# Turning the result tiles of the last output projection on VectorE instead of TensorE

## The chip, the core and the metric

The kernel runs on one core of one Trainium2 chip. The metric is the device time of one execution in microseconds (us), as the median of several executions. The engines named below are TensorE (PE, with its weight loads shown apart as PEld), VectorE (DVE), ScalarE (ACT), GpSimd (POOL) and SyncE (SP). SP computes nothing here: it issues transfers (DMAs). ACT issues some as well.

## The reference, cut to what matters

One step of a two-layer decoder trunk on 1024 new prompt tokens and on 8 sample tokens. Layer 0 is a retention layer, layer 1 a sliding-window attention layer. Each layer ends with an output projection and a residual; the change concerns that of layer 1, which gives the outputs y_prompt and y_sample.

```python
def swa_layer(x, g_norm, w_in, q_gain, k_gain, sinks, w_out, k_buf=None, v_buf=None):
    B, L, _ = x.shape
    h = rmsnorm(x, g_norm)
    proj = h @ w_in
    q, k, v, gate = jnp.split(proj, [SWA_Q, SWA_Q + SWA_KV, SWA_Q + 2 * SWA_KV], axis=-1)
...
    o = o * jax.nn.silu(gate)
    return x + o @ w_out, new_k, new_v
```

Here x is 1024 x 1024 for the prompt and 8 x 1024 for the sample, and w_out is 1024 x 1024, all in fp32.

## The kernel before

**Tiles.** The gated branch output of the attention layer lies in the on-chip tensor `SA`, with features on the partitions and 1032 tokens (1024 of the prompt, 8 of the sample) along the free axis. Its product with w_out is made in 24 result tiles (ft, ti). ft counts eight groups of 128 output features, ti three groups of tokens, `TG` = 0 to 384, 384 to 768 and 768 to 1032; the last has 256 prompt and 8 sample tokens. `so_all` (L2173) takes the tiles in the order (0,0) to (5,0), (0,1) to (5,1), (0,2) to (5,2), then (6,0), (6,1), (6,2), (7,0), (7,1), (7,2).

**One tile.** `start` (L2177) asks for weights and for the residual, takes a PSUM buffer (`ms`, `pj` or `sc`) and issues the products of the first seven of eight k steps through `proj` (L1654); `finish` (L2209) issues those of the eighth. To keep fp32 precision every operand is split into a high and a low part, and each k step is three matmuls (L1661 high by high, L1662 high by low, L1663 low by high), so 24 matmuls a tile, with 128 features as outputs and the tile's 384 or 264 tokens as columns. Then `finish` adds the residual on DVE (L2217: `yt`, in a buffer named `sq` with two copies), lets `x_ahead` (L2195) issue the next load of a residual tile, and calls `so_y` for the tile before this one (`pend_y`).

**Turning and storing.** A result tile has features on the partitions, the output has tokens as rows. `so_y` (L2156) turns each 128 tokens by a matmul with the identity (`tr`, L105, into the PSUM buffer `tr`), three of them a tile of 384 tokens; a tile with ti = 2 has two of 128 and one for the 8 sample columns. ACT copies the result to SBUF (`yo`, L2166, and L2170 for the sample) and issues the store on its own queue (L2167 and L2171). Each row of that store is one run of 128 features, 512 bytes.

**Residuals.** `x_ahead` loads residual tile `xr2` on SP (L2205); where ti = 2 a second, small load brings the 8 sample columns (L2207, from `xdec`). Two buffers exist. The load for a tile can be issued when the add of the tile two before it has read its buffer.

**Weights.** `wslot` (L1638) loads 256 columns of w_out, that is the weights of two groups ft, in two halves of 512 KB on SP (L1647, into `wr`), and splits them: ACT writes the high part (`wh`, L1650), DVE at this place subtracts for the low part (`wl`, L1651). There are three buffers of `wh` and `wl` for four pairs of groups. The last pair (ft 6 and 7) therefore goes into the buffer of the first (ft 0 and 1), whose last reader is tile (1,2), six tiles and a part before its first use in (6,0).

**What sets the order.** PE's instructions stand in the order in which the program issues them. In this part of the kernel the order on DVE, ACT and SP is decided by a scheduler, which places instructions by its own estimates of when they can run; so an edit can move instructions that it doesn't name. On each engine, instructions and transfers are issued strictly in order: one that waits holds up all behind it. The hardware transfers raise eight semaphores in turn, and each transfer waits for the one that used its semaphore before, eight transfers earlier.

Of the kernel before, what the change touches and what calls it, by code (L numbers as in the profile page):

```python
# [7 lines left out]
F32 = mybir.dt.float32  # L8
F32R = mybir.dt.float32r
AF = mybir.ActivationFunctionType  # L10
# [60 lines left out]
def _trunk(ctx, tc, nc, a):  # L71
# [6 lines left out]
    y_p, y_s, nrp, nrs = a["y_p"], a["y_s"], a["nrp"], a["nrs"]  # L78
# [25 lines left out]
    def tr(out, in_, ident, start=True, stop=True):  # L104
        nc.tensor.matmul(out, in_, ident, is_transpose=True, start=start, stop=stop)  # L105


    ident = cp.tile([128, 128], F32, name="ident")
# [601 lines left out]
    t0 = 0.0  # L710
    for h in range(H):
        t0 = max(t0 + GAP, sets[3 * h + 2].end + 10.0)
# [209 lines left out]
    trp = ctx.enter_context(tc.tile_pool(name="trp", bufs=2, space=PSUM))  # L922
# [797 lines left out]
    atp = ctx.enter_context(tc.tile_pool(name="atp", bufs=1))  # L1720
# [115 lines left out]
    def dec_cache(hf):  # L1836

        pt = trp.tile([128, 512], F32, name="tr")
        for i in range(4):
            tr(pt[:, i * 128:i * 128 + 128], kcT["c"][:, 4 * hf + i, :], ident)  # L1840
        return pt
# [314 lines left out]
    def so_y(ft, ti, yt):  # L2156
        t0, t1 = TG[ti]
        npr = min(t1, NP) - t0
        nch = npr // 128
        pt = trp.tile([128, 512], F32, name="tr")  # L2160
        for i in range(nch):
            tr(pt[:, i * 128:i * 128 + 128], yt[:, i * 128:i * 128 + 128], ident)
        if ti == 2:
            tr(pt[:8, 256:384], yt[:, 256:264], ident)
        yo = atq[0].tile([128, 384], F32, tag="ot", name="yo", bufs=2)
        nc.scalar.activation(yo[:, :npr], pt[:, :npr], AF.Copy)  # L2166
        nc.scalar.dma_start(out=y_p[0, t0:t0 + npr, ft * 128:ft * 128 + 128].rearrange("(c p) f -> p c f", p=128),  # L2167
                            in_=yo[:, :npr].rearrange("p (c f) -> p c f", f=128))
        if ti == 2:
            nc.scalar.activation(yo[:8, 256:384], pt[:8, 256:384], AF.Copy)  # L2170
            nc.scalar.dma_start(out=y_s[:, 0, ft * 128:ft * 128 + 128], in_=yo[:8, 256:384])  # L2171

    def so_all():  # L2173
# [35 lines left out]
        def finish():  # L2209
            ft, ti, ps = early.pop(0)  # L2210
            held.discard(min(held))
            t0, t1 = TG[ti]
            n = t1 - t0
            proj(ps[:, :n], so_slots[ft // 2], ft % 2, t0, t1, first=False, last=True, ks=[7])
            yield 3 * n / 2400.0
            yt = io("sq", 2)
            nc.vector.tensor_tensor(yt[:, :n], ps[:, :n], xrs.pop(0)[:, :n], ALU.add)  # L2217
            x_ahead()
            if pend_y:
                so_y(*pend_y.pop(0))  # L2220
            pend_y.append((ft, ti, yt))
# [11 lines left out]
        while pend_y:  # L2233
            so_y(*pend_y.pop(0))
# [13 lines left out]
    out = so_all()  # L2248
# [53 lines left out]
    pt = dec_cache(0)  # L2302
# [4 lines left out]
    pt = dec_cache(1)  # L2307
# [100 lines left out]
```

## Time and profile before

| quantity | value |
| --- | --- |
| time, median of 3 runs | 1294.03 us (1293.03 to 1294.62) |
| the profiled execution's own time | 1293.47 us |
| its span in the profile | 1291.7 us |
| mean granted TensorE clock over the span | 0.996 of full speed |
| DVE, ACT, POOL busy over the span | 766.3, 668.2, 741.4 us |
| first and last add of the output projection (L2217) | 1182.4 and 1287.2 us |
| loads of residual tiles, 16 and 8 | 192 KB and 128 KB each, by SP |
| stores of result tiles, 16 and 8 | 192 KB and 128 KB each, by ACT |

Times in the trace are in us from the start of the span, and 1.8 us of the execution's own time lie outside it. A row of a timeline gives start, duration, engine, line, operation and output<-inputs; a bracket behind it is the idle time of that engine just before, and what ended it. PE's matmuls are pipelined: the distance from one start to the next says what one costs, not its duration.

### The profile page before, as it was taken

The page shows a single profiled execution, that of the slowest core. Times are in us where ns is not written, and L with a number is a line of the kernel's source. Part 1 is how long each engine was busy: PE and PEld are TensorE (multiplying, and loading weights), DVE is VectorE, ACT ScalarE, POOL GpSimd, SP SyncE. Part 2 cuts the span into 40 slices and gives each one's busy share as a digit, 9 for nine tenths or more (in the row PEclk, how much of TensorE's full clock was granted, in tenths as well). Part 3 has the DMA queues.
Part 4 walks back from the last instruction along what each step waited for, and adds up shares of the span by engine and source line. Part 5 has one row for each costly group of instructions (what it writes and reads, how often), then busy time and mean ns, then how long its engine had stood idle before and what let it go on. Part 6 is the DMA issues. An engine that isn't in the chain of part 4 may idle for free.

```text
span 1291.7 us, 26846 instructions
## 1 busy us (share of the span) xinstructions
PE 1268.1 (98%) x9839; PEld 1216.2 (94%) x9839; DVE 766.3 (59%) x1474; ACT 668.2 (52%) x1656; POOL 741.4 (57%) x886
## 2 busy tenths in 40 slices
PE   6999999999999999999999999999999999999998
PEld 5999999999999999988889999999999999998998
DVE  5954646665576764476763656855566666765321
ACT  5533445454555554588761234545575766765121
POOL 5654444535359899798771458636585767544000
PEclk9999999999999999999999999999998999999999
DMA  6313857677667673556879855833031221137232
GB/s 227 108 54 121 253 183 237 179 253 218 186 210 226 192 239 107 180 173 218 255 211 261 229 195 153 272 113 103 15 118 50 66 66 58 54 119 249 78 92 79
DMA packets 221967, 206.69 MB, mean 160 GB/s; under 512 B 32728, under 2 KB 196820, under 8 KB 221820
## 3 DMA queue, kind: packets, MB, share of 16 engines
q1 hardware_dynamic: 189840, 170.61, 43.8%
q10 hardware_dynamic: 31996, 34.36, 8.2%
q8 instruction: 78, 1.28, 0.4%
q14 instruction: 53, 0.43, 0.1%
HBM read 135.41 MB, written 70.55 MB: 159 GB/s over the span
## 4 chain that ended last, share of the span: by engine, by line
PE 90%; DVE 3%; DMA 2%; POOL 1%; ACT 1%; issue 1%; SPq 0%; ACTq 0%; DVEq 0%; POOLq 0%
PE b L335 8%; PE b L336 8%; PE b L337 8%; PE S L1302 7%; PE pj L1661 6%; PE pj L1662 6%; PE pj L1663 6%; PE b L328 4%; PE tr L105 4%; PE b L329 4%; PE b L330 4%; PE o L2023 2%; PE b L544 1%; PE sc L1986 1%; PE S L335 1%; PE S L336 1%
## 5 line engine op out<-in xcount | busy, mean ns | idle before, releaser
L335 PE MATMUL b<-xh,woh 128*128 128x258 f32 x784 | 223.2, 285 | 0.0
L337 PE MATMUL b<-xh,wol 128*128 128x258 f32 x784 | 221.7, 283 | 0.0
L336 PE MATMUL b<-xl,woh 128*128 128x258 f32 x784 | 221.6, 283 | 0.0
L1661 PE MATMUL pj<-SA,wh 128*128 128x384 f32 (+1 forms) x496 | 169.3, 341 | 1.5 <-ACT SA L2043 1.3
L1662 PE MATMUL pj<-SA,wh 128*128 128x384 f32 (+1 forms) x496 | 159.4, 321 | 0.2 <-DVE SA L2044 0.2
L1663 PE MATMUL pj<-SA,wl 128*128 128x384 f32 (+1 forms) x496 | 159.4, 321 | 0.0
L335 PEld LDWEIGHTS b<-xh,woh 128*128 128x128 f32 x784 | 148.0, 189 | 4.1 <-issue 3.7
L336 PEld LDWEIGHTS b<-xl,woh 128*128 128x128 f32 x784 | 148.7, 190 | 0.0
L337 PEld LDWEIGHTS b<-xh,wol 128*128 128x128 f32 x784 | 148.0, 189 | 0.0
L226 POOL TENSOR_TENSOR wol<-raw,woh 128x512 fp32r<-128x512 f32 x51 | 66.2, 1306 | 120.3 <-ACT woh L221 109.2
L328 PE MATMUL b<-woh,xh 128*128 128x256 f32 x448 | 126.6, 283 | 0.0
L329 PE MATMUL b<-wol,xh 128*128 128x256 f32 x448 | 126.0, 281 | 0.0
L330 PE MATMUL b<-woh,xl 128*128 128x256 f32 x448 | 125.6, 280 | 0.0
L1661 PEld LDWEIGHTS pj<-SA,wh 128*128 128x128 f32 x496 | 94.1, 190 | 5.1 <-issue 2.4
L1662 PEld LDWEIGHTS pj<-SA,wh 128*128 128x128 f32 x496 | 94.3, 190 | 0.4 <-DVE SA L2044 0.4
L2001 POOL TENSOR_TENSOR s<-s,sm 128x512 f32<-128x512 f32 x64 | 66.6, 1041 | 48.2 <-DVE sm L2000 43.2
L1663 PEld LDWEIGHTS pj<-SA,wl 128*128 128x128 f32 x496 | 93.9, 189 | 0.0
L328 PEld LDWEIGHTS b<-woh,xh 128*128 128x128 f32 x448 | 84.3, 188 | 5.0 <-issue 2.9
L330 PEld LDWEIGHTS b<-woh,xl 128*128 128x128 f32 x448 | 84.3, 188 | 0.0
L329 PEld LDWEIGHTS b<-wol,xh 128*128 128x128 f32 x448 | 84.3, 188 | 0.0
L1993 ACT ACTIVATE s<-s,mx 128x257 f32<-128x257 f32 x128 | 64.2, 505 | 34.9 <-DVE mx L1991 34.2
L221 ACT ACTIVATE woh<-s 128x512 fp32r<-128x512 f32 x88 | 54.1, 624 | 54.4 <-POOL s L211 20.7
(530 smaller groups left out, 3622.6 us busy)
## 6 DMA issues: line engine op xcount, KB each, us to landing
raw<-in_w_in_ret_dram ACTq DMA_DIRECT2D x44, 512.0 KB
st<-in_state_ret_dram SPq DMA_DIRECT2D x64, 256.0 KB
out_dram<-st SPq DMA_DIRECT2D x64, 256.0 KB
vb<-vscr SPq DMA_DIRECT2D x64, 128.0 KB
evp<-qks SPq DMA_DIRECT2D x32, 256.0 KB
evx<-vsc SPq DMA_DIRECT2D x32, 256.0 KB
wr<-in_w_in_swa_dram SPq DMA_DIRECT2D x32, 256.0 KB
evc<-gsc SPq DMA_DIRECT2D x16, 256.0 KB
```

The source lines that it names most:

```text
L226: eng.tensor_tensor(lo, src_of(s, name, sub), hi.bitcast(F32), SUB)
L328: mm(dst, xh, wh, start=a and i == 0, stop=False, skip_group_check=True)
L329: mm(dst, xh, wl, start=False, stop=False, skip_group_check=True)
L330: mm(dst, xl, wh, start=False, stop=z, skip_group_check=True)
L335: mm(dst, wh, xh, start=a, stop=False, **sg)
L336: mm(dst, wh, xl, start=False, stop=False, **sg)
L337: mm(dst, wl, xh, start=False, stop=z, **sg)
L1302: mm(box[0], s.op[f"A{i + 1}{j + 1}", 0][w][:, k, :], xs_[t][x[j]][:, k, :], start=(xs_ is XH and w == 0 and j + k == 0), stop=(xs_ is XL ...
L1661: mm(ps, hi[:, k, fs], xh[:, k, t0:t1], start=first and k == ks[0], stop=False)
L1662: mm(ps, hi[:, k, fs], xl[:, k, t0:t1], start=False, stop=False)
L1663: mm(ps, lo[:, k, fs], xh[:, k, t0:t1], start=False, stop=last and k == ks[-1])
L2001: nc.gpsimd.tensor_tensor(st[:, :, 0:256], st[:, :, 0:256], sm.unsqueeze(2).broadcast_to([128, 2, 256]), ALU.mult)
```

## The change

`so_y` takes another way for all tiles but (7,1) and (7,2), which are stored last. DVE turns `yt` with one instruction, which transposes every 32x32 block in place of its own, into a buffer `ptf` with four copies. After that, partition 32q + r of `ptf` holds, for each block b of 32 tokens, the 32 features 32q to 32q + 31 of token 32b + r. Four transfers on SP's queue store the four groups q, each with 32 partitions of 12 (ti = 2: 8) runs of 32 numbers, 128 bytes. For ti = 2 the 8 sample columns are still turned by PE, copied by ACT and stored by ACT. (7,1) and (7,2) keep the old way.

```diff
         t0, t1 = TG[ti]
         npr = min(t1, NP) - t0
         nch = npr // 128
+        if (ft, ti) not in ((7, 1), (7, 2)):
+            yo = atp.tile([128, 512], F32, name="ptf", bufs=4)
+            nc.vector.transpose(yo[:, :npr], yt[:, :npr])
+            for q in range(4):
+                f0 = ft * 128 + 32 * q
+                nc.sync.dma_start(out=y_p[0, t0:t0 + npr, f0:f0 + 32].rearrange("(b r) c -> r b c", r=32),
+                                  in_=yo[32 * q:32 * q + 32, :npr].rearrange("r (b c) -> r b c", c=32))
+            if ti == 2:
+                pt = trp.tile([128, 512], F32, name="tr")
+                tr(pt[:8, 256:384], yt[:, 256:264], ident)
+                nc.scalar.activation(yo[:8, 256:384], pt[:8, 256:384], AF.Copy)
+                nc.scalar.dma_start(out=y_s[:, 0, ft * 128:ft * 128 + 128], in_=yo[:8, 256:384])
+            return
         pt = trp.tile([128, 512], F32, name="tr")
         for i in range(nch):
             tr(pt[:, i * 128:i * 128 + 128], yt[:, i * 128:i * 128 + 128], ident)
```

Lines behind the edit have a number 13 higher in the changed kernel (the add is L2230 there, the residual's loads L2218 and L2220); its transposes are L2162, its four stores L2165.

The scheduler gives the changed kernel another order. On DVE, before, at the place where the weights of the last pair are split (`wl_16437`); the adds here are those of (5,1) into `sq_16195`, (0,2) into `sq_16232`, (1,2) into `sq_16269` and (2,2) into `sq_16308`:

```order
L2217 TENSOR_TENSOR sq_16195<-pm_16170,xr2_16168 128x384 [waits DMAHW2_49,PE_49]
L2217 TENSOR_TENSOR sq_16232<-pj_16207,xr2_16204 128x264 [waits DMAHW7_49,DMAHW6_49,PE_49]
L2217 TENSOR_TENSOR sq_16269<-pj_16244,xr2_16241 128x264 [waits DMAHW0_49,DMAHW2_49,DVE_49,PE_49]
L1651 TENSOR_TENSOR wl_16437<-wr_16438,wh_16436 128x512 [waits DMAHW3_49,Activation_49]
L1651 TENSOR_TENSOR wl_16437<-wr_16438,wh_16436 128x512 [waits Activation_49]
L1651 TENSOR_TENSOR wl_16437<-wr_16444,wh_16436 128x512 [waits DMAHW4_49,Activation_49]
L2217 TENSOR_TENSOR sq_16308<-pm_16283,xr2_16280 128x264 [waits DMAHW3_49,DMAHW5_49,DVE_49,PE_49]
```

The same place on DVE in the changed kernel; the adds are those of (4,1) into `sq_16150`, (5,1) into `sq_16185`, (0,2) into `sq_16221` and (1,2) into `sq_16257`, the last pair's low part is `wl_16430`:

```order
L2230 TENSOR_TENSOR sq_16150<-pj_16108,xr2_16106 128x384 [waits DMAHW5_49,PE_49]
L2162 STREAM_TRANSPOSE ptf_16187<-sq_16150 128x384 [waits DMAHW2_49,DMAHW7_49,DMAHW1_49,DVE_49]
L1651 TENSOR_TENSOR wl_16430<-wr_16431,wh_16429 128x512 [waits PE_49,Activation_49]
L1651 TENSOR_TENSOR wl_16430<-wr_16431,wh_16429 128x512 [waits Activation_49]
L2230 TENSOR_TENSOR sq_16185<-pm_16160,xr2_16158 128x384 [waits DMAHW2_49]
L2162 STREAM_TRANSPOSE ptf_16223<-sq_16185 128x384 [waits DMAHW6_49,DMAHW7_49,DMAHW4_49,DVE_49]
L2230 TENSOR_TENSOR sq_16221<-pj_16196,xr2_16193 128x264 [waits DMAHW7_49,DMAHW0_49]
L2162 STREAM_TRANSPOSE ptf_16259<-sq_16221 128x256 [waits DMAHW3_49,DMAHW4_49,DMAHW1_49,DVE_49]
L2230 TENSOR_TENSOR sq_16257<-pj_16232,xr2_16229 128x264 [waits DMAHW7_49,DMAHW6_49]
```

The first two `wl`, which wait for PE's last use of the first pair's buffer in (1,2), stood behind the add of (1,2) and now stand ahead of the adds of (5,1) and (0,2).

On SP, before, from the residual of (5,1) (`xr2_16168`) over those of (0,2) (`xr2_16204`) and (1,2) (`xr2_16241`):

```order
L2205 DMA xr2_16168<-xscr_67 128x384 [waits DMAHW7_49,DVE_49]
L1647 DMA wr_16444<-in_w_out_swa_dram 128x4x256 [waits DMAHW4_49,PE_49]
L2205 DMA xr2_16204<-xscr_67 128x256 [waits DMAHW6_49,DMAHW0_49,DVE_49]
L2207 DMA xr2_16204<-xdec_70 128x8
L2205 DMA xr2_16241<-xscr_67 128x256 [waits DMAHW2_49,DVE_49]
```

On SP in the changed kernel, from the residual of (5,2) (`xr2_16389`) over the stores of (4,2) (`ptf_16419`) to the first store of (5,2) (`ptf_16472`); `xr2_16443` is the residual of (6,0):

```order
L2218 DMA xr2_16389<-xscr_67 128x256 [waits DMAHW2_49]
L2220 DMA xr2_16389<-xdec_70 128x8 [waits DMAHW3_49]
L2165 DMA out_0_dram<-ptf_16419 32x8x32 [waits DMAHW4_49,DVE_49]
L2165 DMA out_0_dram<-ptf_16419 32x8x32 [waits DMAHW5_49]
L2165 DMA out_0_dram<-ptf_16419 32x8x32 [waits DMAHW6_49]
L2165 DMA out_0_dram<-ptf_16419 32x8x32 [waits DMAHW7_49]
L1647 DMA wr_16437<-in_w_out_swa_dram 128x4x256 [waits DMAHW0_49,PE_49]
L2218 DMA xr2_16443<-xscr_67 128x384 [waits DMAHW1_49]
L2165 DMA out_0_dram<-ptf_16472 32x8x32 [waits DMAHW2_49,DVE_49]
```

The load of the last half of the last pair's weights stood ahead of the residual of (0,2) and now stands behind the four stores of (4,2).

On SP in the changed kernel, from the residual of (0,2) (`xr2_16193`) to the first store of (0,2) (`ptf_16259`), with the stores of (5,1) (`ptf_16223`) and the residual of (1,2) (`xr2_16229`):

```order
L2218 DMA xr2_16193<-xscr_67 128x256 [waits DMAHW7_49]
L2220 DMA xr2_16193<-xdec_70 128x8 [waits DMAHW0_49]
L2165 DMA out_0_dram<-ptf_16223 32x12x32 [waits DMAHW1_49,DVE_49]
L2165 DMA out_0_dram<-ptf_16223 32x12x32 [waits DMAHW2_49]
L2165 DMA out_0_dram<-ptf_16223 32x12x32 [waits DMAHW3_49]
L2165 DMA out_0_dram<-ptf_16223 32x12x32 [waits DMAHW5_49]
L2218 DMA xr2_16229<-xscr_67 128x256 [waits DMAHW6_49]
L2220 DMA xr2_16229<-xdec_70 128x8 [waits DMAHW7_49]
L2165 DMA out_0_dram<-ptf_16259 32x8x32 [waits DMAHW0_49,DVE_49]
```

Between the residual loads of two tiles, which followed each other directly on SP, there now stand the four stores of an earlier tile, the first of which waits for DVE's transpose.

## The prediction, made before the changed kernel was run

> **What bounds the kernel now.** I read the page first: span, busy time by engine, the chain that ended last.
>
> ```profile
> span 1291.7 us, 26846 instructions
> PE 1268.1 (98%) x9839; PEld 1216.2 (94%) x9839; DVE 766.3 (59%) x1474; ACT 668.2 (52%) x1656; POOL 741.4 (57%) x886
> PE 90%; DVE 3%; DMA 2%; POOL 1%; ACT 1%; issue 1%; SPq 0%; ACTq 0%; DVEq 0%; POOLq 0%
> ```
>
> PE is busy for 98% of the span and makes 90% of the chain. But shares are means over stages, and the change touches one stage alone. So next I read the busy time by windows; 1180 to 1291 is that stage, the others serve below.
>
> ```profile
> core 0: us, PE busy (x) PEld busy (x) DVE busy (x) ACT busy (x) POOL busy (x), PEclk, DMA share, GB/s
> 967.60:971.00 3.40, 0.64 (x6) 0.42 (x4) 0.72 (x1) 1.27 (x3) 3.40 (x6) 1.00 0.29 75
> 971.00:977.80 6.80, 6.63 (x25) 6.63 (x26) 5.37 (x14) 5.49 (x16) 4.35 (x6) 0.50 0.27 97
> 1237.30:1240.60 3.30, 3.30 (x12) 3.30 (x11) 0.65 (x3) 0.83 (x3) 0.00 (x0) 0.50 0.81 248
> 685.00:696.00 11.00, 11.00 (x93) 11.00 (x92) 2.83 (x8) 0.00 (x0) 0.00 (x0) 1.00 1.02 194
> 1180.00:1291.00 111.00, 106.68 (x734) 103.79 (x734) 27.18 (x53) 23.34 (x62) 6.35 (x10) 0.98 0.36 105
> ```
>
> In the stage PE is busy 106.68 of 111 us, DVE 27.18, ACT 23.34. Whatever shortens PE's work shortens the span, as long as no other engine holds PE up; and ACT's copies and stores, off the path, are worth nothing when they go. DVE and the DMAs have room on the mean. So the question is what one transpose costs PE, and whether the new order makes PE wait.
>
> **What PE gains.** Starts on PE's timeline, at a tile of 384 tokens and at the start of one of 264:
>
> ```profile
> 1266.50 0.34 PE L1662 MATMUL pj<-SA,wh 128*128 128x384 f32 x1
> 1266.68 0.33 PE L1663 MATMUL pj<-SA,wl 128*128 128x384 f32 x1
> 1266.85 0.49 PE L105 MATMUL tr<-ident,sq 128*128 128x128 f32 x3
> 1267.09 0.42 PE L1661 MATMUL pj<-SA,wh 128*128 128x384 f32 x1
> 1267.36 0.34 PE L1662 MATMUL pj<-SA,wh 128*128 128x384 f32 x1
> 1271.83 0.28 PE L1662 MATMUL pm<-SA,wh 128*128 128x264 f32 x1
> 1271.95 0.28 PE L1663 MATMUL pm<-SA,wl 128*128 128x264 f32 x1
> ```
>
> A matmul of 384 columns costs a step of 0.175 us, one of 264 columns 0.12. The three transposes push the next start by 0.24 (1266.85 to 1267.09), and the matmul after them has a step of 0.27 in place of 0.175, so 0.09 more: 0.335 a tile, about 0.08 for each transpose plus 0.09 once. Of the 22 changed tiles 15 lose three transposes: 15 x 0.335 = 5.0. Seven with ti = 2 lose two of three and keep the small one with its 0.09: 7 x 0.165 = 1.2. The **gain is 6.2 us**.
>
> **What DVE and SP get.** DVE's groups by form and SP's timeline give the nearest rows:
>
> ```profile
> L1234 DVE STREAM_TRANSPOSE evx<-xr 128x256 f32<-128x256 f32 x4 | 1.6, 402 | 0.0
> L1122 DVE STREAM_TRANSPOSE ra<-ra 128x128 f32<-128x128 f32 x2 | 0.5, 284 | 0.0
> ```
>
> ```profile
> 683.32 2.34 SPq L1225 DMA_DIRECT2D xr<-in_x_prompt_dram  x4
> 685.75 2.02 SPq L1225 DMA_DIRECT2D acc<-in_x_prompt_dram  x4
> 1246.69 0.32 SPq L2205 DMA_DIRECT2D xr<-xscr  x1
> 1247.06 0.42 SPq L2207 DMA_DIRECT2D xr<-xdec  x1
> ```
>
> The same operation takes 0.28 us on 128 columns and 0.40 on 256, so I estimate 0.53 on 384. 15 x 0.53 + 7 x 0.40 = 10.8 us on DVE, which has 84 us idle in the stage: hidden, except where it stands between a wait and what PE needs. The new stores have no row; the nearest are the four transfers of L1225, which also have 32 partitions and many short runs (256 bytes): 2.02 to 2.34 for four, with the gaps 0.5 to 0.6 each. I take **0.45 for one**, between the 0.37 of L2205 to L2207 and 0.6. 22 x 4 x 0.45 = 40 us on SP, mostly in its idle time too.
>
> **What is moved: loss 1.** Call E the moment at which PE ends tile (1,2), just ahead of its add at 1249.48 in DVE's timeline; ACT's row of the high weights follows.
>
> ```profile
> 1249.48 0.43 DVE L2217 TENSOR_TENSOR sq<-pj,xr 128x264 f32<-128x264 f32 x1 [2.82 <-PE pj L1663]
> 1250.02 0.69 DVE L1651 TENSOR_TENSOR wl<-wr,wh 128x512 fp32r<-128x512 f32 x1
> 1251.86 1.29 DVE L1651 TENSOR_TENSOR wl<-wr,wh 128x512 fp32r<-128x512 f32 x2 [1.14 <-ACT wh L1650]
> 1267.05 0.56 DVE L2217 TENSOR_TENSOR sq<-pj,xr 128x384 f32<-128x384 f32 x1 [4.10 <-PE pj L1663]
> ```
>
> ```profile
> 1249.36 0.63 ACT L1650 ACTIVATE wh<-wr 128x512 fp32r<-128x512 f32 x1 [2.31 <-DMA out_dram<-yo]
> ```
>
> In the new order the first two `wl` stand on DVE ahead of the adds of (5,1) and (0,2). They need PE's last read of the first pair's buffer, at E. Behind the small transpose of (0,2), for which PE needs the add of (0,2), stands all of tile (2,2). From E: `wh` to `wl` 0.66 (1249.36 to 1250.02), two `wl` 1.29, add of (5,1) 0.56, its transpose 0.53, add of (0,2) 0.43 = **3.5 us** in which PE waits. Every term has a row; the only doubt is whether the last four run into one another by 0.1.
>
> **Loss 2.** The transpose of (5,1) is done at E + 3.0. Then SP: four stores to 4.8, the residual of (1,2), its sample part issued from 5.2. How long a load takes to land has no clean row in this stage. The chain of waits has loads and small stores:
>
> ```profile
> 685.17 3.69 DMA xr<-in_x_prompt_dram
> 693.83 4.83 DMA rb<-in_w_out_ret_dram
> 888.55 3.25 DMA wr<-in_w_in_swa_dram
> 1168.76 3.01 DMA ms<-ms
> ```
>
> I take 3.0, the shortest of the four: a residual is 128 KB here, the 3.25 moved 256 KB, and the 3.69 moved 128 KB in runs of 256 bytes, at the full DMA share of the window from 685. 3.7 stands above it, and below it 2.3: ACT's row above lays its wait to 1249.36 to a store issued at 1247.08.
>
> ```profile
> 1247.08 0.42 ACTq L2167 DMA_DIRECT2D out_dram<-yo  x1
> ```
>
> So the add of (1,2) starts at E + 8.2 and ends at 8.6. PE, set free at 3.5, needs 0.17 + 24 x 0.12 = 3.05 for the transpose and (2,2), and waits at the small transpose of (1,2) from 6.5 to 8.6: **2.1 us** (1.4 by landings of 2.3, 2.8 by 3.7).
>
> **Loss 3.** From there the adds follow their residuals, and these SP's queue. With the same terms: stores of (1,2) 9.0 to 10.8, of (2,2) 11.6 to 13.4, residual of (4,2) behind them, landed 16.8, added and turned by 17.6, stores of (4,2) to 19.4. Only then SP issues the last half of the last weights, which before stood on SP ahead of the residual of (0,2), twelve microseconds ahead of E:
>
> ```profile
> 1236.85 0.38 SPq L1647 DMA_DIRECT2D wr<-in_w_out_swa_dram  x1
> ```
>
> It lands 3.25 later (up to 4.83, as the 512 KB of row 693.83 did), `wh` takes 0.66: E + 23.3. PE makes (3,2), (4,2) and (5,2) without another wait, 3.05 each, starts (6,0) at 17.9 and needs that half at its fifth k step, 12 x 0.175 = 2.1 later, at 20.0. It waits 3.3, and 0.35 more at the third matmul, until `wl` (0.69) follows `wh`: **3.6 us** (2.9 and 5.9 by the short and the long landings).
>
> **Loss 4, the clock.** PE's rows at the granted clock of 0.50:
>
> ```profile
> 1239.07 0.52 PE L1662 MATMUL pm<-SA,wh 128*128 128x384 f32 x1
> 1239.39 0.52 PE L1663 MATMUL pm<-SA,wl 128*128 128x384 f32 x1
> ```
>
> In the windows above, 3.4 us with PE busy only 0.64 were followed by 6.8 us at a clock of 0.50. Losses 1 and 3 are two idle stretches of about that length. At half clock a step is 0.32 instead of 0.175, so a stretch of 3.4 us costs 3.4 x (1 - 0.175/0.32) = 1.55. Whether an idle time triggers one depends on where it falls; I count one of the two: **1.55** (none 0, both 3.1), and leave the one at 1237, ahead of all this, as it is.
>
> **The sum**: -6.2 + 3.5 + 2.1 + 3.6 + 1.55 = +4.55. On the profiled execution's 1293.47 (span 1291.7 and 1.8 outside) that is 1298.0; it lies 0.56 below the median 1294.03, so the forecast for a median is **1298.6**.
>
> **Rivals.** A measurement of this kernel tells about 0.2%, 2.6 us, from no change: "same" is 1291.4 to 1296.6.
>
> *About the same.* Landings of 2.3 give losses of 3.5 + 1.4 + 2.9 = 7.8, and if neither idle time slows the clock the sum is +1.6: 1295.7. For it speaks that the clock's drop isn't certain; against it, that both idle stretches are as long as the one that was followed by it.
>
> *The other side: faster.* The group of transposes in this stage:
>
> ```profile
> L105 PE MATMUL tr<-ident,sq 128*128 128x128 f32 (+1 forms) x72 | 11.8, 273 | 0.3 <-DVE sq L2217 0.3
> ```
>
> If each transpose taken away were worth its recorded 273 ns, 15 x 3 + 7 x 2 = 59 of them would bring 16.1 in place of 6.2: 1294.0 - 16.1 + 9.2 + 1.55 = 1288.7. It decides from (9.2 + 1.55)/59 = 0.18 us a transpose on. Against it: starts lie 0.08 apart, so durations overlap. The Trainium skill, "TensorE: Matmul & The Clock Gate", section "Part 4: PE-mode transpose", gives about 275 ns for one transpose in one kernel's context. The recorded 273 ns agree as a duration; the starts show that the next doesn't wait for it, and so I give this rule little chance.
>
> *Small stores land late.* A tile with ti = 2 has seven transfers, and a transfer waits for the one eight before it. As long as a landing is under 8/7 of PE's 3.05 a tile, 3.5 us, nothing queues. At 6 us a tile takes 7/8 x 6 = 5.25; over the five tiles (1,2) to (5,2) 5 x 2.2 = 11 us in place of the 2.1 of loss 2, so 1307. For it: runs are only 128 bytes. Against it: window 685 to 696 moved 194 GB/s, mostly in runs of 256 bytes, at a share of 1.02; at the same cost a run, 128 bytes give 97 GB/s, and a tile's 128 KB take 1.4 of its 3.05 us. It decides from about three times that cost. The Trainium skill, "DMA: Bandwidth & Descriptors", section "Specifications", says that below 512 bytes the engine reads, modifies and writes; by an estimate that doubles a run's cost it would be 2.7 of 3.05 us, tight but no queue. No run here shows stores that short.
>
> **How the numbers follow.** Forecast, slower by the reordering: 0.66. About the same: 0.20. Faster: 0.05. Late stores: 0.09. Slower in all 0.66 + 0.09 = 0.75. The range goes from 1293.5, under the short landings without a clock drop, to 1304, just above the long landings with both drops (-6.2 + 3.5 + 2.8 + 5.9 + 3.1 = +9.1, 1303.2); the faster rival and the late stores are left out.
>
> **What would show it.** Right: no `tr` of three between matmuls of 384; PE idle about 3.5 us ahead of (2,2), laid to the add or DVE; idle again ahead of (3,2); idle about 3.6 us inside (6,0), laid to `wh`; a stretch of half clock after one of them. SP's load of `wr` in the last 25 us before (6,0) ends, not 12 us ahead of (1,2). Wrong: if PE runs through (2,2) without idling, if the last half's load finds SP free early, or if a store takes over 3.5 us to land.

## The result and the profile after

The changed kernel takes 1299.47 us (median of 5 runs, 1298.42 to 1300.87), the kernel before 1293.32 (median of 5, 1291.77 to 1294.62; three of the five are the runs behind the 1294.03 given ahead). The ratio is 1.0049, with an interval of 1.0037 to 1.0061: 6.3 us slower. The profiled execution of the changed kernel took 1300.87, the slowest of the five, with a span of 1299.0. Single executions of one kernel differ by some us, in step with the granted clock: of 20 executions of the kernel before, measured beside some of the experiments, the five with a mean granted clock of 0.999 took 1291.25 to 1292.92 us, the others, at 0.996 or 0.997, 1293.15 to 1295.92.

The page of the changed kernel, span, busy time and the chain by engine:

```profile
span 1299.0 us, 26799 instructions
PE 1266.7 (98%) x9780; PEld 1214.1 (93%) x9780; DVE 778.5 (60%) x1496; ACT 658.3 (51%) x1634; POOL 739.5 (57%) x886
PE 91%; DVE 2%; DMA 2%; POOL 2%; issue 1%; SPq 1%; ACT 1%; ACTq 0%; DVEq 0%; POOLq 0%
```

PE is busy for 1.4 us less than before, and the span is 7.3 us longer: PE was not given more to do, it waited or ran slower. Neither shows in its share, which is 98% as before. What PE waited for in the stage, by the view of waits (engine, line, releaser: us in total, times, longest):

```profile
PE pj L1661 <- ACT wh L1650: 4.4, 1, 4.4
PE tr L105 <- DVE sq L2230: 4.4, 3, 3.4
```

Both are new, but for 0.3 us of the second at the last tile. The wait of 3.4 us on PE's timeline, from the end of (1,2) over (2,2):

```profile
1245.40 0.28 PE L1663 MATMUL pj<-SA,wl 128*128 128x264 f32 x1
1249.10 0.37 PE L105 MATMUL tr<-ident,sq 128*8 128x128 f32 x1 [3.42 <-DVE sq L2230]
1249.13 0.57 PE L1661 MATMUL pm<-SA,wh 128*128 128x264 f32 x1
1249.49 0.42 PE L1662 MATMUL pm<-SA,wh 128*128 128x264 f32 x1
...
1254.55 0.42 PE L105 MATMUL tr<-ident,sq 128*8 128x128 f32 x1
1254.62 0.47 PE L1661 MATMUL pj<-SA,wh 128*128 128x264 f32 x1
1254.93 0.28 PE L1662 MATMUL pj<-SA,wh 128*128 128x264 f32 x1
...
1258.54 0.27 PE L105 MATMUL tr<-ident,sq 128*8 128x128 f32 x1 [0.66 <-DVE sq L2230]
```

PE ends (1,2) at 1245.68 and stands idle at the small transpose of (0,2) for 3.42 us. Then the 24 matmuls of (2,2) come in steps of 0.22 us, where one of 264 columns cost 0.12 before. DVE's timeline says what the transpose waited for:

```profile
1246.26 1.29 DVE L1651 TENSOR_TENSOR wl<-wr,wh 128x512 fp32r<-128x512 f32 x2 [8.56 <-ACT wh L1650]
1247.47 0.55 DVE L2230 TENSOR_TENSOR sq<-pm,xr 128x384 f32<-128x384 f32 x1
1248.06 0.58 DVE L2162 STREAM_TRANSPOSE ptf<-sq 128x384 f32<-128x384 f32 x1
1248.56 0.40 DVE L2230 TENSOR_TENSOR sq<-pj,xr 128x264 f32<-128x264 f32 x1
...
1253.44 0.43 DVE L2230 TENSOR_TENSOR sq<-pj,xr 128x264 f32<-128x264 f32 x1 [4.01 <-DMA xr<-xdec]
```

DVE stood idle for 8.56 us at the two subtractions, with the add of (5,1) ready behind them; then come, in the new order, subtractions, add and transpose of (5,1), add of (0,2). The add of (1,2) then waits for its residual until 1253.44. The wait inside (6,0) on PE's timeline, and the chain of waits ahead of it (start, us, what; SPq is SP's issuing):

```profile
1271.36 0.44 PE L1661 MATMUL pj<-SA,wh 128*128 128x384 f32 x1 [4.38 <-ACT wh L1650]
1271.64 0.33 PE L1662 MATMUL pj<-SA,wh 128*128 128x384 f32 x1
1272.08 0.69 PE L1663 MATMUL pj<-SA,wl 128*128 128x384 f32 x1
```

```profile
1255.30 2.94 DMA out_dram<-ptf
1258.25 0.34 SPq L2218
1258.64 0.43 SPq L2220
1259.17 0.38 SPq L2165
...
1266.53 0.46 SPq L2165
1267.09 0.40 SPq L1647
1267.53 3.14 DMA xr<-xscr
1270.68 0.64 ACT wh L1650
1271.34 0.70 DVE wl L1651
1272.08 0.69 PE pj L1663
```

From 1258.25 to 1267.53 the chain is nothing but SP issuing, one transfer right behind another, residuals and stores, until the load of the weights (L1647) gets its turn. (The row at 1267.53 names the next transfer, a residual's; what `wh` reads is the weights, whose load was issued at 1267.09.) The wait at its head, 1255.30 to 1258.25, is for ACT's small store of sample rows (L2171), eight transfers ahead of the residual's load: a short wait, 0.7 us on SP. The windows with a lower clock, and the stage:

```profile
1234.40:1237.80 3.40, 3.40 (x13) 3.40 (x12) 2.71 (x7) 0.39 (x3) 0.00 (x0) 0.50 0.07 10
1249.10:1254.60 5.50, 5.50 (x26) 5.42 (x27) 1.21 (x3) 0.27 (x1) 0.00 (x0) 0.50 0.50 86
1271.80:1275.20 3.40, 3.29 (x11) 3.12 (x11) 0.83 (x2) 0.02 (x1) 0.00 (x0) 0.52 0.05 18
1180.00:1299.00 119.00, 105.15 (x675) 101.54 (x675) 38.27 (x76) 14.21 (x40) 6.46 (x10) 0.94 0.45 99
```

Behind each of the two waits PE ran at half clock. The stretch at 1234.4 stands ahead of both; it is the one that before has at 1237, and the prediction left it in. The mean of the stage fell from 0.98 to 0.94.

### The profile page after: what moved, and what is told of

Its sections match the earlier page's. It is cut to its first block, busy times and chain, and to the rows that moved or that the text cites. A ratio compares the mean times of both kernels' runs of the same rounds, so it can differ in the third digit from the quotient of the medians.

```text
span 1299.0 us, 26799 instructions
## 1 busy us (share of the span) xinstructions
PE 1266.7 (98%) x9780; PEld 1214.1 (93%) x9780; DVE 778.5 (60%) x1496; ACT 658.3 (51%) x1634; POOL 739.5 (57%) x886
## 4 chain that ended last, share of the span: by engine, by line
PE 91%; DVE 2%; DMA 2%; POOL 2%; issue 1%; SPq 1%; ACT 1%; ACTq 0%; DVEq 0%; POOLq 0%
PE S L1302 9%; PE b L335 8%; PE b L336 8%; PE b L337 8%; PE pj L1661 6%; PE pj L1663 6%; PE pj L1662 5%; PE b L328 4%; PE b L329 4%; PE b L330 4%; PE tr L105 4%; PE o L2023 2%; PE b L544 1%; PE sc L1986 1%; PE S L335 1%; PE S L336 1%
```

## Experiments

The theory: the transposes' gain on PE is 6.2 us; it is eaten by two places at which an in-order queue was rearranged (DVE's subtractions ahead of adds, SP's weight load behind stores), and by the half clock behind the two idle times. The rival: the stores of 128-byte runs cost the time themselves, by their issue, their landing or their load on the DMAs. A difference in us is the ratio to the kernel before on the same chip, times its median.

Two columns are read from one traced execution of each kernel. "PE's stage" is the time from PE's first product of the output projection (1181.12 before) to its last group of transposes (1287.73 before), less the 106.61 us that this takes before. The last column says whether the half clock near 1237, which before has, is there; where it is missing, 1.55 us of a difference are not the edit's own terms.

| run | edit | ratio to before, 95% interval | us | PE's stage, us | half clock near 1237 |
| --- | --- | --- | --- | --- | --- |
| (the change) | | 1.0049, 1.0037 to 1.0061 | +6.3 | +7.0 | yes |
| e1_pool | last subtractions on POOL | 1.0024, 1.0015 to 1.0033 | +3.1 | +2.1 | no |
| e2_wract | last weights loaded by ACT | 0.9993, 0.9985 to 1.0002 | -0.9 | -0.9 | no |
| e3_poolwr | both | 0.9965, 0.9953 to 0.9978 | -4.5 | -5.4 | no |
| e4_notr | before, transposes left out | 0.9953, 0.9939 to 0.9967 | -6.1 | -6.5 | yes |
| e5_actq | stores issued by ACT | 1.0049, 1.0034 to 1.0065 | +6.3 | +4.7 | yes |
| e6_xract | residuals loaded by ACT | 1.0029, 1.0016 to 1.0042 | +3.8 | +3.8 | yes |
| e7_all | e3 and e6 | 0.9951, 0.9938 to 0.9965 | -6.3 | -8.0 | no |
| e8_ti01 | 12 tiles of 22 | 0.9998, 0.9989 to 1.0007 | -0.3 | +0.9 | no |
| e9_last | e7, (7,0) the old way | 0.9948, 0.9931 to 0.9966 | -6.7 | -7.6 | no |

**e1_pool: the subtractions off DVE.**

```diff
     def so_ahead(n):
         for fp in range(len(so_slots), n):
+            eng, lo_eng[0] = lo_eng[0], (nc.gpsimd if fp == 3 else lo_eng[0])
             so_slots[fp] = wslot(w_out_swa[:, fp * 256:fp * 256 + 256], False)
+            lo_eng[0] = eng
```

> The changed kernel with one edit: the low part of the last pair of weights is computed on POOL instead of DVE, so nothing of it stands ahead of the adds of (5,1) and (0,2). By my theory PE's idle time of 3.42 us ahead of tile (2,2) falls under 0.5 us, and the half clock behind it goes too; the idle time inside (6,0), whose load of weights stays behind the stores of (4,2), stays at 4 to 5 us, with one half-clock stretch. Sum against before: -6.2 + 4.6 + 1.6 = 0, so between -1.5 and +1.5 us. The rival, that the 128-byte stores themselves (their issue on SP, their landing, their share of the DMAs) cost the time, expects it to stay at +5 to +7 us, as in the changed kernel.

Measured +3.1 us. PE's waits in this run, and two windows:

```profile
PE pj L1661 <- ACT wh L1650: 4.2, 1, 4.2
PE tr L105 <- DVE sq L2232: 2.2, 4, 1.2
PE pj L1663 <- POOL wl L1651: 0.3, 1, 0.3
```

```profile
1182.00:1261.00 79.00, 76.97 (x535) 74.67 (x534) 29.27 (x59) 10.60 (x32) 7.97 (x9) 1.00 0.49 105
1265.50:1271.80 6.30, 5.94 (x18) 5.25 (x19) 1.14 (x2) 0.74 (x2) 2.50 (x2) 0.52 0.08 27
```

The 3.4 us are gone, and with them the half clock at that place; the wait for the weights stands, as expected. So DVE's order made the first wait. The size missed the expectation: the adds now wait for residuals behind stores (2.2 us in four waits, 0.3 of them at the end as before, the longest 1.2), which I had left out; and the half clock behind the weights lasted 6.3 us instead of 3.4, 6.3 x (1 - 0.175/0.32) = 2.9 us. Up to 1261 the clock is full, so before's own stretch at 1237 (1.55) is not there. -6.2 + 1.9 + 4.2 + 0.3 + 2.9 - 1.55 = +1.55, where PE's stage grew by 2.1 in the trace; the rest of the +3.1 I can't place.

**e2_wract: the weight load off SP.**

```diff
-                nc.sync.dma_start(out=raw, in_=src[512 * j:512 * j + 512].rearrange("(k p) f -> p k f", p=128))
+                (nc.scalar if len(so_slots) == 3 else nc.sync).dma_start(out=raw, in_=src[512 * j:512 * j + 512].rearrange("(k p) f -> p k f", p=128))
```

> The changed kernel with one edit: the two loads of the last pair of weights are issued on ACT's queue instead of SP's, so no store stands ahead of them. By my theory the idle time inside (6,0) goes (under 0.5 us). The scheduler now places three of the four low-part subtractions ahead of the add of (0,2), so the idle time ahead of (2,2) grows from 3.4 to 4.1 to 4.8 us and the half clock behind it stays (2.5 us). Sum against before: -6.2 + 4.5 + 2.5 + 0.7 = +1.5, so between 0 and +3 us. The rival of the costly stores expects +5 to +7 us.

Measured -0.9 us, 0.9 under the range expected. PE's wait and the windows ahead of it and behind it:

```profile
PE tr L105 <- DVE sq L2230: 4.8, 2, 4.5
```

```profile
1182.00:1242.70 60.70, 60.70 (x412) 59.05 (x411) 21.40 (x42) 6.62 (x20) 4.53 (x7) 1.00 0.49 111
1247.20:1252.60 5.40, 5.38 (x27) 5.37 (x28) 1.23 (x3) 0.27 (x1) 0.00 (x0) 0.54 0.54 100
```

The wait inside (6,0) is gone, the wait ahead of (2,2) is 4.5 us, as the order says, and 5.4 us at half clock follow. What the expectation lacked is again the stretch at 1237, which this run doesn't have: -6.2 + 4.5 + 2.4 - 1.55 = -0.85, what was measured.

**e3_poolwr: both edits.**

> The changed kernel with both edits: low part of the last pair on POOL, its loads on ACT's queue. The four stores of each tile stay on SP, 128 bytes a run. By my theory neither idle time is left but one of about 1.3 us at the small transpose of (0,2), and no new half clock: -6.2 + 1.3 = -5 us against before, between -3.5 and -6.5. The rival of the costly stores expects it no faster than before (0 to +3 us).

Measured -4.5 us. All 88 stores are still on SP, 128 bytes a run. PE's waits and the stage:

```profile
PE tr L105 <- DVE sq L2232: 2.3, 3, 1.4
```

```profile
1181.00:1284.00 103.00, 99.26 (x675) 96.15 (x675) 35.58 (x71) 13.58 (x38) 11.43 (x14) 1.00 0.50 111
```

Without the two long waits there is no half clock at all. 2.0 us of waits are left besides the 0.3 at the end: adds whose residual stands behind stores. The half clock of before at 1237 is not there either, so the terms are -6.2 + 2.0 - 1.55 = -5.75, and PE's stage is 5.4 us shorter in the trace. The rival of costly stores falls: it expected no gain, and even without the 1.55 about 3 us are left of the -4.5.

**e4_notr: the price of the transposes.** In this kernel the prompt rows of the 22 tiles are stored unturned.

```diff
-        pt = trp.tile([128, 512], F32, name="tr")
+        pt = trp.tile([128, 512], F32, name="tr") if (ti == 2 or (ft, ti) == (7, 1)) else None
+        old = (ft, ti) in ((7, 1), (7, 2))
-        for i in range(nch):
+        for i in range(nch if old else 0):
             tr(pt[:, i * 128:i * 128 + 128], yt[:, i * 128:i * 128 + 128], ident)
...
-        nc.scalar.activation(yo[:, :npr], pt[:, :npr], AF.Copy)
+        nc.scalar.activation(yo[:, :npr], (pt if old else yt)[:, :npr], AF.Copy)
```

> The kernel before with TensorE's 128-token transposes taken out of the 22 tiles and nothing in their place: ACT copies the sum itself instead of the turned one, and the stores stay as before. The prompt rows of these 22 tiles are therefore stored unturned. It prices the 59 transposes alone. By my theory, steps between starts, -6.2 us against before (between -5.5 and -7). By their recorded mean of 273 ns each, -16 us. If PE were held by something else at these places, 0.

Measured -6.1 us (-7.9 to -4.3). The steps between starts price a transpose, its recorded duration (-16) doesn't.

**e5_actq: the stores on another queue.**

```diff
-                nc.sync.dma_start(out=y_p[0, t0:t0 + npr, f0:f0 + 32].rearrange("(b r) c -> r b c", r=32),
+                nc.scalar.dma_start(out=y_p[0, t0:t0 + npr, f0:f0 + 32].rearrange("(b r) c -> r b c", r=32),
```

> The changed kernel with one edit: the four stores of each tile are issued on ACT's queue instead of SP's. SP's order is then that of before, with the last half of the weights loaded ahead of the residual of (1,2). But ACT's own work now stands behind the stores, which wait for DVE's transposes: the high part of the last pair is placed behind the stores of (4,2). By my theory the waits move with the queue: no idle time of 3.4 us ahead of (2,2), but waits of 0.5 to 1.5 us at the sample attention, ahead of (0,2) and at the small transposes of (2,2) and (3,2), and 5 to 6.5 us at the start of (6,0). Sum against before: -6.2 + 4.5 + 6 + 1.6 to 3.1 = +6 to +8 us. A theory in which only SP's queue is too full expects -4 to -6 us.

Measured +6.3 us. PE's new waits:

```profile
PE pj L1661 <- ACT wh L1650: 4.6, 1, 4.6
PE o L2121 <- DVE pm L2109: 1.5, 1, 1.5
PE tr L105 <- ACT ptf L2170: 1.1, 2, 0.8
PE pj L1661 <- DVE SA L2130: 0.8, 1, 0.8
```

On SP the last half of the weights is loaded early again, at 1234.58 us, and nothing is won: the stores wait on ACT's queue for DVE's transposes, and ACT's splitting of the weights and its copies stand behind them. The waits have moved with the queue. The total came as expected, but not all of it is accounted for: the four waits, 8.0 us, and one half clock behind the longest give -6.2 + 8.0 + 1.55 = +3.35, PE's stage is 4.7 us longer in the trace, and the traced execution, 1298.36 us, is the fastest of six.

**e6_xract: the residuals off SP.**

```diff
-            nc.sync.dma_start(out=xr[:, :npr], in_=xscr[ft // 2, xp_, :, t0:t0 + npr].rearrange("p u t -> (p u) t"))
+            nc.scalar.dma_start(out=xr[:, :npr], in_=xscr[ft // 2, xp_, :, t0:t0 + npr].rearrange("p u t -> (p u) t"))
             if ti == 2:
-                nc.sync.dma_start(out=xr[:, npr:n], in_=xdec[ft // 2, xp_].rearrange("p u t -> (p u) t"))
+                nc.scalar.dma_start(out=xr[:, npr:n], in_=xdec[ft // 2, xp_].rearrange("p u t -> (p u) t"))
```

> The changed kernel with one edit: the loads of residual tiles are issued on ACT's queue instead of SP's, so they no longer stand behind stores. The scheduler then puts the first two low-part subtractions behind the add of (1,2), on DVE as before the change; the last half of the weights stays on SP behind the stores of (4,2). By my theory there is no idle time ahead of (2,2) and (3,2), with nothing moved to POOL, and the whole wait is inside (6,0): PE comes there earlier, the load no earlier than PE's pace lets it, so 8 to 9 us. Sum against before: -6.2 + 9 + 1.6 to 3.1 = +4.5 to +6 us. If DVE's subtractions themselves and not their place held PE up, the 3.4 us would stay ahead of (2,2) or (3,2).

Measured +3.8 us. PE's wait, and DVE's timeline at the subtractions:

```profile
PE pj L1661 <- ACT wh L1650: 8.4, 1, 8.4
```

```profile
1245.20 0.43 DVE L2230 TENSOR_TENSOR sq<-pj,xr 128x264 f32<-128x264 f32 x1 [2.02 <-PE pj L1663]
1245.75 0.69 DVE L1651 TENSOR_TENSOR wl<-wr,wh 128x512 fp32r<-128x512 f32 x1
```

This is the cleanest test of the first place: the same subtractions on the same engine, behind the add of (1,2) instead of ahead of the add of (5,1), and PE has no wait there. (The residual loads moved too. In the changed kernel they were not what held up the adds of (5,1) and (0,2): SP had issued them by 1238.59 and 1241.96, and the add of (5,1) starts right behind the subtractions, without a gap.) Everything is now inside (6,0). With one half-clock stretch behind it, -6.2 + 8.4 + 1.55 = +3.75; the expectation had counted a longer wait and up to two stretches.

**e7_all: e3 and e6 together.**

> The changed kernel with three edits: low part of the last pair on POOL, its loads on ACT's queue, the residual loads on ACT's queue. SP has only the stores left. By my theory no wait is left and the whole gain shows: -6.2 + 0.2 = -6 us against before, between -5 and -7, the same as the transposes alone, and 1 to 1.5 us below the version with two edits. The rival of the costly stores expects it above the run without transposes by 2 us or more.

Measured -6.3 us (-8.0 to -4.5), as much as the transposes alone brought in e4. No wait of PE is left in the stage but those of before. The stage, and one row of SP's waits:

```profile
1181.00:1281.00 100.00, 98.71 (x675) 96.16 (x675) 35.77 (x70) 13.66 (x40) 10.68 (x12) 1.00 0.50 110
```

```profile
SPq L2167 <- DMA out_dram<-yo: 5.4, 1, 5.4
```

The second row is a surprise. A store of (7,0) on SP waited 5.4 us for a store of (7,1) on ACT, a later tile, because the eight semaphores are handed out in the scheduler's order, across queues. PE's last matmul ended at 1280.52, and the span at 1286.1: 5.6 us, where it is 3.4 before. So the total is made of three terms, not one: the transposes, the half clock at 1237 that this run lacks, and 2.2 us more at the end, -6.2 - 1.55 + 2.2 = -5.55. That it equals the -6.1 of e4 so closely is partly luck. What rules the costly stores out is PE's stage: 8.0 us shorter, where the first two terms give 7.75, with all 88 stores in it.

**e8_ti01: twelve tiles only.**

```diff
-        if (ft, ti) not in ((7, 1), (7, 2)):
+        if ti < 2 and ft < 6:
```

> The change for the 12 tiles with ft under 6 and ti under 2 alone; the tiles of ti = 2 and of ft 6 and 7 are turned by TensorE as before. The gain is 12 x 0.335 = 4.0 us. On DVE the first two low-part subtractions still stand ahead of the adds of (5,1) and (0,2), so the idle time of 3.4 us ahead of (2,2) and the half clock behind it (2.5 us) stay; the last half of the weights is loaded behind the residual of (2,2), with no store ahead of it, so the idle time inside (6,0) goes. Sum against before: -4.0 + 3.4 + 2.5 = +1.9 us, between +0.5 and +3.5. The rival of the costly stores, with 48 of 88 stores left, expects half of the changed kernel's loss or more, +3 us, but with no idle time of 3.4 us at that place.

Measured -0.3 us (-1.4 to +0.9). PE's wait and the window behind it:

```profile
PE tr L105 <- DVE sq L2230: 3.7, 2, 3.4
```

```profile
1246.10:1252.00 5.90, 5.88 (x27) 5.82 (x28) 0.43 (x1) 0.53 (x2) 0.00 (x0) 0.50 0.73 150
```

The 3.4 us stand at their place with 48 of the 88 stores, none of them of ti = 2, and the wait inside (6,0) is gone: the first wait is the order's, not the stores' number. The expectation missed by the stretch at 1237, which this run lacks: -4.0 + 3.4 + 2.6 - 1.55 = +0.45, against -0.3 measured and +0.9 in PE's stage.

**e9_last: the tail of e7.** Of e7, with one line changed:

```diff
-        if (ft, ti) not in ((7, 1), (7, 2)):
+        if ft < 7:
```

> The version with three edits, and tile (7,0) also turned by TensorE and stored by ACT as before. In the run with three edits three of the four stores of (7,0) were issued on SP only at 1282.39 us and after, 2 us behind the last matmuls, because a transfer waits for the one eight before it and the scheduler had counted ACT's store of (7,1), issued at 1280.27, among those. Without stores of (7,0) on SP nothing on SP waits for ACT's last stores. The transposes of (7,0) cost PE 0.34 us again. Sum against the version with three edits: +0.3 - 2.0 = -1.7 us, so -7.5 to -8 us against before. If the end were set by anything else, +0.3 us.

Measured -6.7 us against before, 1286.15 us in place of 1292.74, somewhat short of the -7.5 expected. The interval overlaps that of e7, so the times alone don't tell the two apart. The traces do: PE's last matmul ends at 1279.48 and the span at 1283.1, 3.6 us behind it, 2.0 less than in e7; and PE's stage is 0.35 us longer than in e7, the price of three transposes. It is the fastest version measured, by its median, and beats both kernels.

## Why the prediction was right

It said slower, 1298.6 us, and by the reordering; 1299.47 was measured, and the mechanism is the one described. By its steps:

- **Gain 6.2.** Right: -6.1 where the transposes alone were taken out.
- **Loss 1, 3.5.** Right in place and size: 3.42 us at the small transpose of (0,2), with the five steps in the order foreseen. It went with the subtractions (e1) and with their place in the order (e6, in which the residual loads left SP as well), and not with 40 of the stores (e8).
- **Loss 2, 2.1.** The mechanism is there, the size was not: 0.66 us of waiting in the changed kernel. The add of (1,2) started 7.8 us behind PE's end of (1,2) (8.2 in the prediction; SP issued the last part of its residual at 1251.41, 0.5 us later than forecast, and the add started 2.0 us after that, where I took 3.0 for a landing). But PE ran (2,2) at half clock and came 2.5 us late itself, so the residual was in time. Two losses that I added lay beside each other. Where the half clock is absent, as in e3, 2.0 us of such waits show.
- **Loss 3, 3.6.** Right in place, too small: 4.38 us, and 0.27 more at the third matmul (1271.64 to 1272.08 instead of a step of 0.175), 4.65. SP issued the load at 1267.09 and `wh` began at 1270.68, 3.6 us where I took 3.25; the four stores of a tile took SP 1.85 to 1.95 us, up to 0.49 each in place of 0.45, and SP lost 0.7 us to the semaphore of ACT's small store.
- **Loss 4, 1.55.** Too small. The stretch at 1237 stayed, as forecast. But both idle times were followed by half clock, not one: 5.5 us in which (2,2) took 5.4 instead of 24 x 0.12 = 2.9, so 2.5, and 3.4 us at (6,0), 1.55. Together 4.05.

The sum of what the trace shows: -6.2 + 3.4 + 0.7 + 4.65 + 4.05 = +6.6 of the 7.0 by which PE's stage grew; 0.4 isn't placed, and the other 0.3 of the 7.3 between the two spans lie outside the stage. Against the forecast's +4.55 that is 2.05 more: the clock's price was under-counted by 2.5 and loss 3 by 1, while loss 2 was over-counted by 1.4. Between the two medians lie 6.15 us, 1.6 more than forecast; the traced execution was the slowest of the five. The direction and the places are the prediction's own merit. That 1298.6 came within 0.9 us of 1299.47 owes something to luck: errors of opposite sign partly cancelled, and the kernel before came out 0.7 us lower in its five runs than in the three from which the forecast starts.

The rivals: the faster one falls by e4. The late stores fall by e3 and e7, in which all 88 stores stay and PE's stage shrinks by 5.4 and 8.0 us. In the changed kernel SP hardly waited for a landing: before its wait at the program's end, 0.7 us for a residual's and 0.7 us for this one, which is ACT's small store of sample rows (it reads `ptf` too), so none for a store of 128-byte runs.

```profile
SPq L2218 <- DMA out_dram<-ptf: 0.7, 1, 0.7
```

The short runs do take more of the DMAs: the windows of the stage show 110 GB/s at a share of 0.50 in e7, and 105 GB/s at 0.36 before. There was room for that.

DVE's transposes cost what the rows of before said, or little more (estimates 0.53 and 0.40): they were never the question.

```profile
L2162 DVE STREAM_TRANSPOSE ptf<-sq 128x384 f32<-128x384 f32 x15 | 8.5, 572 | 2.7 <-PE o L2023 2.2
L2162 DVE STREAM_TRANSPOSE ptf<-sq 128x256 f32<-128x256 f32 x7 | 3.1, 446 | 0.4
```

## What to carry to other kernels

Work taken off the bounding engine counts only if the queues it is put on don't carry something that engine waits for later: here four small stores a tile pushed a weight load 30 us down an in-order queue. Where a scheduler orders the other engines, read its new order for the few instructions with waits on the far side (a reused buffer, a late load) before looking at busy time; and give such loads and conversions an idle engine and queue of their own. Two losses behind one another may overlap: price the slower clock that follows an idle time first, then ask what it hides. And when a total agrees, add up its terms from the trace before calling it explained: in e7 two terms beside the expected one nearly cancelled.

## What the runs showed of the hardware

- Every idle time of PE of 3.4 us or more in this stage was followed by a granted clock near 0.5, for 3.4 to 6.3 us: 3.42 us by 5.5, 4.38 by 3.4, 4.2 (e1) by 6.3, 4.5 (e2) by 5.4, 4.6 (e5) by 3.5, 3.4 (e8) by 5.9, 8.4 (e6) by 3.4. In e6 the clock fell while PE was still idle (mean 0.80 over the 8.4 us). An idle time therefore cost 1.5 to 2.9 us more than itself. Waits up to 1.4 us (e3) had none behind them.
- Before has one such stretch at 1237 without a long idle time, and so have the change (1234.4), e4, e5 and e6; e1, e2, e3, e7, e8 and e9 have none there. What decides it isn't settled, and it moves a time by 1.55 us, which is a quarter of what the change was to gain.
- A transfer on one queue can wait for one of a later tile on another queue through the shared semaphores: 5.4 us on SP in e7, 2 us at the end of the span. SP's stores in e7 also waited 18.3 us, in 12 waits, for residual loads on ACT's queue; that cost PE nothing.
